# Folding two modulation rows and a gate by adding transfers instead of by sums with ones on TensorE

## Chip, core and metric

One core of one Trainium2 chip runs the program once. The metric is the device time of that run in microseconds (us); for the kernel before it is the median of three runs. The core's engines are TensorE (PE in the profile; its weight loads are PEld), VectorE (DVE), ScalarE (ACT), GpSimd (POOL) and SyncE (SP). Each has its own list of instructions; transfers (DMA) are issued from SP's, ACT's and POOL's lists and move on 16 DMA engines.

## The reference, cut to what matters

A transformer-like layer on 1024 tokens of width 1024 with 256 context tokens, all in float32:

```
mod = silu(c) @ w_mod + b_mod            # one row of 6 * 1024 numbers
sh1, sc1, gt1, sh2, sc2, gt2 = split(mod, 6)
h  = rmsnorm(x, g_pre_mix) * (1 + sc1) + sh1
u, q, k, v = h @ w_in                    # pooling half and attention half
mix = concat(pool_mixer(u), neighbourhood_attention(q, k, v)) @ w_out
x  = x + gt1 * rmsnorm(mix, g_post_mix)
h2 = rmsnorm(x, g_pre_mlp) * (1 + sc2) + sh2
y  = square(relu(h2 @ w_mlp_in)) @ w_mlp_out
out = x + gt2 * rmsnorm(y, g_post_mlp)
```

The rows `gt1`, `sh2`, `sc2` and `gt2` are the ones named "a", "sh", "sc" and "b" in the kernel. Each is a product of a vector of 1024 with a 1024x1024 matrix.

## The kernel before

The products are made of float32 numbers split into a high and a low part (`split`, `high_low`), three matmuls for one (`three`, L226 to L228), and the large products are put together from fewer products of sums of blocks (P1 to P7). In order of time: modulation of the first sub-layer and projection (to about 210 us), attention in 32 units of a head pair and eight columns of tokens (`units`, to about 313 us), the output projection (to about 390), the first MLP product (block pairs `block_pair(p)`, p from 0 to 15, to about 700), the second MLP product (to the end).

**How a modulation row is made.** `mod_begin` takes a page of 128x1024, sets it to zero and loads the bias into its first partition. Eight parts of `w_mod` are loaded, and VectorE adds each, times one column of silu(c), into the page (`mod_add`, L251). The page `acc` then holds for each of the 1024 outputs 128 partial sums, one in each partition, and these have still to be added up. `mod_sums_of` does this on TensorE: four matmuls with a matrix of ones (L264), each for 256 outputs, so that the sums of a quarter stand in 32 partitions of a bank of PSUM. What follows differs:

- "a" and "b", the gates: VectorE multiplies the sums by the gain (`mod_gate`, L275), whose quarters four transfers bring to the same partitions (`mod_gain`, L271). `mod_out` (L281) writes the row to DRAM in four transfers, and `gate_page` (L287) reads it back into all 128 partitions: `Ga` and `Gb`.
- "sc" and "sh", scale and shift of the second sub-layer: ScalarE copies the sums (`column_sums`, L847), `mod_out` writes four quarters, and `columns_of` (L850) reads the row back as 8 columns of 128, into `sc2` and `s2`. From these VectorE makes `a2`, `less_a2` and `less_s2` (L1752 to L1754), which `normal_pair` and `normal_sides` (L1774, L1798, L1800) use on the transposed tokens.

The shift's page is stored to DRAM (`kept_row`, L842) after its last part and loaded into a new page at the first unit of attention (L1489). The sums of "a" and of both modulation rows stand in unit 2 of the attention loop; the transfers out are jobs of units 5 and 6, those of columns jobs of units 10 and 12. The sums of "b" stand ahead of group 3 of the second MLP product's P1; its parts are added in block pairs 10 to 12.

**What sets the order.** A planner orders the instructions of each engine: from its own estimate of times it takes, of those whose inputs are ready, the one that stands first in the program, and it chooses the buffers. `in_order(engines)` fixes the order on the engines named, as written, for what is inside. The attention part and the transfers behind it are such a list on POOL (`first_pool`); the second part of the output projection, from the row steps on, is another (`added`), and nothing ties the two lists to each other. `tc.issue_after(i)` only sets what follows behind instruction i on its own engine. Adding transfers (`add_to`: DRAM or SBUF plus what stands there) are issued from POOL's list. A transfer that needs an earlier one's result waits in its engine's list for that to land.

**Around the change, in the output projection.** POOL's list has: the sums of pairs of weight blocks (`t2`, whose tiles are named to_2w and to_3w, as those of `t3` and `t4`), one sum of head outputs, two adding transfers into `t3` and two into `t4`. Then come the row steps of the first four token tiles: VectorE adds two partial mean squares (`vm`), POOL takes the power -1/2 (`rm`, L168), VectorE makes the new row (L1670), ScalarE its square, POOL a second power (`rn`), and VectorE the scaled row `mp` (L1683), which TensorE transposes (`px`, L1765) for the MLP. `wt3` and `wt4` are the split blocks of `t3` and `t4`.

Of the kernel before, what the change touches and what calls it, by code (L numbers as in the profile page):

```python
# [11 lines left out]
F32 = mybir.dt.float32  # L12
# [6 lines left out]
P = 128  # L19
D = 1024  # L20
KT = D // P
# [87 lines left out]
def hybrid_block(ctx, tc, x, ctx_in, w_mod, mod_pages, w_u, b_mod, gp1, gp2, w_in, pool_w, rpb, w_out, w1, w2, vectors,  # L109
                 mask, edge, out):  # L110
    nc = tc.nc
    sub, mul, add = ALU.subtract, ALU.mult, ALU.add
# [6 lines left out]
    dram = ctx.enter_context(tc.tile_pool(name="dram", bufs=1, space=DRAM))  # L119

    def cst(name, shape, dt=F32):
        return const.tile(shape, dt, tag=name, name=name)
# [4 lines left out]
    def page(name, dt=F32):  # L127
        return act.tile([P, 1024], dt, tag="pg", name=name)
# [85 lines left out]

    def add_to(to, more):
        nc.gpsimd.dma_start(to, more, accum_op=add)  # L216

    def pair(w, kk, c0, n):
        return w[2 * kk * P : (2 * kk + 2) * P, c0 : c0 + n].rearrange("(a p) f -> p a f", p=P)
# [41 lines left out]
    def mod_sums_of(name, acc, bank):  # L261
        ps = bank(f"pg{name}")
        for c in range(4):
            nc.tensor.matmul(ps[32 * c : 32 * c + 32, :256], ones[:, :32], acc[:, c * 256 : (c + 1) * 256],  # L264
                             start=True, stop=True)
        return ps[:, :256]

    def mod_gain(gp, g, queue):
        quarters = gp.rearrange("(c o f) -> c o f", c=4, o=1)
        for c in range(4):  # L270
            queue.dma_start(g[32 * c : 32 * c + 32, :], quarters[c].to_broadcast([32, 256]))  # L271
        return g

    def mod_gate(name, acc, g, bank):
        nc.vector.tensor_tensor(acc[:, :256], mod_sums_of(name, acc, bank), g, mul)  # L275


    def mod_out(name, acc):
        gates[name] = dram.tile([1, D], F32, tag=f"g{name}", name=f"g{name}")
        for c in range(4):  # L280
            nc.gpsimd.dma_start(gates[name][:, c * 256 : (c + 1) * 256], acc[32 * c : 32 * c + 1, :256])  # L281

    gates = {}
# [13 lines left out]
    a2, s2 = cst("a2", [P, KT]), cst("s2", [P, KT])  # L297

    with tc.tile_pool(name="ps1", bufs=6, space=PSUM) as ps1, tc.tile_pool(name="tmp1", bufs=3) as tmp:

        def bank(name):
            if name[:2] == "pm" or name in ("pxt5", "pxb2", "pxb3", "pxb4", "pxb5", "pcs", "pcr"):
                return lasting(name)
            return ps1.tile([P, 512], F32, tag="mm", name=name)
# [526 lines left out]
        accs = {}  # L831


        kept_row = dram.tile([P, D], F32, tag="row", name="row")

        def mod_parts(name, c, n):
            accs[name] = mod_begin(name, c, page)
# [5 lines left out]
                yield  # L843


        def column_sums(name, acc, bank):
            nc.scalar.copy(acc[:, :256], mod_sums_of(name, acc, bank))  # L847

        def columns_of(name, to):
            nc.gpsimd.dma_start(to, gates[name].rearrange("o (k p) -> p (o k)", p=P))  # L850

        scale2 = cst("sc2", [P, KT])
        rest.append(mod_parts("sh", 3, KT))
# [372 lines left out]
    with (  # L1226
# [217 lines left out]
        with in_order(ET.PE, ET.Activation, ET.DVE, ET.SP) as projected:  # L1444
# [16 lines left out]
            def right_added(j):  # L1461
# [4 lines left out]
            built = lambda j: next(table[j])  # L1466
            out_of = lambda n: mod_out(n, accs[n])
            jobs = {0: [(built, 1), (key_parts, 1, 0), (key_parts, 1, 1)], 1: [(built, 1)], 2: [(built, 1)], 3: [(built, 1)],
                    4: [(built, 1)], 5: [(out_of, "a"), (out_of, "sc")], 6: [(out_of, "sh")], 7: [(query_parts, 1, 1, True, True)],
                    8: [(mixed_split, 0, True)], 9: [(built, 2)],  # L1470
                    10: [(columns_of, "sc", scale2), (built, 2)], 12: [(columns_of, "sh", s2), (built, 2)],
                    13: [(built, 2), (built, 2)], 14: [(query_parts, 3, 0, False, True)],
                    16: [(mixed_split, 1, True)], 17: [(query_parts, 2, 1, True, True)],
                    18: [(built, 3), (key_parts, 3, 0, False, True)], 20: [(built, 3), (built, 3)],
# [4 lines left out]
            for i in range(N):  # L1479
                if i in LOADS:  # L1480
                    weight_load(0, kks[LOADS.index(i)])
                if i == N - 2:
                    G1 = gate_page("a")
                if i > 3:
                    weighed(i - 4)
                if i == 0:
                    gain = mod_gain(gp1, att.tile([P, 256], F32, tag="gp", name="gpa"), nc.sync)
                    accs["sh"] = page("accsh2")
                    nc.sync.dma_start(accs["sh"], kept_row)  # L1489
                if i == 2:  # L1490
                    mod_gate("a", accs["a"], gain, rest_of_bank)
                if i in (5, 6):
                    for k in (2 * i - 10, 2 * i - 9):
                        nc.sync.dma_start(sa2[k], s3[k])
                low()
                scores(i)
                biased(i, 0)
                if i < N - 1:
                    biased(i, 1)
                if 8 < i and i % 8 == 3:  # L1500
                    right_added(i // 8 - 1)
                if 8 < i and i % 8 == 7:
                    add_to(heads[i // 8 - 1][:, :512], sa2[i // 8 - 1])
                for f, *args in jobs.get(i, ()):
                    f(*args)
                if block_copies and (i < 4 or 6 < i):
                    block_copied()
                for _ in range(SUMS.count(i)):
                    block_summed()
                if i == 2:  # L1510
                    late_query = part_page("qP0_1", False)
                    qparts[0, 1] = late_query[:, :512], late_query[:, 512:]
                    high_part(qT[0][1], qparts[0, 1][0])
                if i > 1:
                    turn(i - 2)
                    fifth_kept(i - 2)
                if i == 2:
                    turn_kept(0, 0, nc.scalar.copy)
                    column_sums("sc", accs["sc"], lambda name: pa[:, :256])
                if i == N - 1:  # L1520
                    turn_kept(i - 2, 0, nc.scalar.copy)
                    turn_kept(i - 2, 1, nc.vector.tensor_copy)
                    biased(i, 1)
                exps(i, 0)
                if i == 2:
                    column_sums("sh", accs["sh"], rest_of_bank)
                if 2 < i < N - 1:
                    turn_kept(i - 2, 0, nc.scalar.copy)
                exps(i, 1)
                if i == 0:  # L1530
                    key_parts(2, 0, True, "lo")
                    key_parts(2, 1, True, "lo")
                    query_parts(2, 0, False, "lo")
                if 1 < i < N - 1:
                    turn_kept(i - 2, 1, nc.vector.tensor_copy)
                if i == 2:
                    low_part(qT[0][1], *qparts[0, 1])
                for filler in fillers.get(i, ()):
                    last_query(*filler)
                if i > 2:  # L1540
                    values(i - 3)
# [60 lines left out]
            for i in range(2):  # L1602
                add_to(t2[i], t1[i])
            add_to(heads[3][:, :512], sa2[3])
            for i in range(2):
                add_to(halved(t3[i]), out_block(i, 1))
            for i in range(2):
                add_to(t4[i], t2[i])
            first_pool.__exit__(None, None, None)
            wt1 = [high_low(f"to1_{t}", t1[t]) for t in range(2)]  # L1610
            junk = lambda t: att.tile([P, NKEY], F32, tag="sp", name=f"jo0_{t}", bufs=6)[:, :512]
# [10 lines left out]
    with tc.tile_pool(name="ps2", bufs=6, space=PSUM) as ps2:  # L1622
# [6 lines left out]
      with ExitStack() as tmp2:  # L1629
# [119 lines left out]

        less_a2, less_s2 = sm("na2", 8), sm("ns2", 8)  # L1750
        with tc.issue_after(projected[ET.DVE]):
            nc.vector.scalar_tensor_tensor(a2, scale2, 1.0, g2c, add, mul)  # L1752
            nc.vector.tensor_scalar_mul(less_a2, a2, -1.0)
            nc.vector.tensor_scalar_mul(less_s2, s2, -1.0)  # L1754
# [521 lines left out]
        with in_order(ET.Pool):  # L2276
            for p in range(1, NPAIR - 1):
                block_pair(p, lambda: acc_b.extend(islice(row_b, 1 if p >= EARLY else 0)))
        assert next(row_b, None) is None
        first_order.__exit__(None, None, None)  # L2280
        fixed.append(True)
        with tc.issue_after(first[ET.PE]), in_order(ET.PE, ET.Activation, ET.DVE, ET.SP, ET.Pool):
# [65 lines left out]
                ending.append((m, gated(m, h, src, True), xt))  # L2348


            pg = bank("pgb")
            inner_banks, parts = {}, {}
            by_two = lambda v: v.rearrange("p (t n) -> p t n", t=2)

# [48 lines left out]
            for name, g in items[: items.index(("P6", 0))]:  # L2403
                if name[0] == "M":
                    inner_group(name, g)
                elif name == "P1":
                    if g == 1:
                        gain = mod_gain(gp2, page("gpb")[:, :256], nc.gpsimd)
                    if g == 3:
                        mod_gate("b", acc_b[-1], gain, lambda name: pg)  # L2410
                        mod_out("b", acc_b[-1])
                    group(x, "P1", g)
                    if g == NG - 1:
                        s1 = halves("s1")
                        for t in range(4):
                            nc.scalar.copy(s1[t], x[t])
                else:
                    group(x, "P2", g, more=True)
                    if g == NG // 2:
                        G2 = gate_page("b")  # L2420
# [110 lines left out]
```

## Time and profile before

| | |
|---|---|
| runs | 1010.14, 1011.23, 1011.56 us; median 1011.23 |
| profiled execution | 1010.35 us, span 1008.6 us |
| TensorE's granted clock | 0.998 of full speed |
| DMA queues | q1 (issued by SP) 181.63 MB, q0 (by POOL) 38.45 MB, q10 (by ACT) 30.97 MB |

The profile shows one execution. The span runs from the first to the last instruction. A row of a timeline has the start, the duration, engine, line, operation, the tile written and those read (`out<-in`, buffer numbers left out), the shape and a count; in brackets the idle time before it and what ended it. In the chain, the work that ended last is followed back, and its pieces don't overlap. "Landing" is the time from a transfer's issue until its data have arrived. The names of tiles: pa, pz and pgb are PSUM banks, S the scores, accsc, accsh and accb the pages of partial sums, gsc and gsh the rows in DRAM, rb the reciprocals of the softmax sums.

### The profile page before, as it was taken

The numbers are of one execution on the slowest core, as the hardware profiler recorded it, in microseconds if no ns is written. First come the engines' busy times: TensorE is split into PE (matmuls) and PEld (weight loads), VectorE is DVE, ScalarE is ACT, GpSimd is POOL, SyncE is SP. The second block draws the span as 40 slices with busy tenths as digits, with TensorE's granted clock in tenths as the row PEclk, the third lists the DMA queues.
The fourth block names the chain that finished last, engine by engine and source line by source line (L and its number), as shares of the span: only waits on it lengthen the run. The fifth ranks groups of instructions, "written<-read, shape, count | busy, mean of one in ns | idle before, by whom it ended". The sixth has DMA issues, their size and how long they took to land.

```text
span 1008.6 us, 16695 instructions
## 1 busy us (share of the span) xinstructions
PE 997.9 (99%) x6062; PEld 829.4 (82%) x6062; DVE 798.6 (79%) x1276; ACT 581.0 (58%) x1038; POOL 201.9 (20%) x278
## 2 busy tenths in 40 slices
PE   8999999999999999999999999999999999999997
PEld 5788888878998888888888888888888888888886
DVE  5589766968885689879998888754798888888895
ACT  6673254448886746786555544545556565544551
POOL 4111110166985232410000000000001000021121
PEclk9999999999999999999999999999999999999999
DMA  9999798665989979986776666625999999579944
GB/s 362 396 278 340 237 273 306 219 160 194 230 184 249 238 191 274 297 208 205 261 252 217 201 215 221 213 89 184 333 371 300 286 341 322 171 220 315 318 166 162
DMA packets 146882, 252.10 MB, mean 250 GB/s; under 512 B 10417, under 2 KB 76849, under 8 KB 146801
## 3 DMA queue, kind: packets, MB, share of 16 engines
q1 hardware_dynamic: 111024, 181.63, 52.9%
q0 software_dynamic: 18640, 38.45, 19.8%
q10 hardware_dynamic: 17136, 30.97, 8.3%
q8 instruction: 47, 0.77, 0.3%
q14 instruction: 35, 0.28, 0.1%
HBM read 197.52 MB, written 69.22 MB: 264 GB/s over the span
## 4 chain that ended last, share of the span: by engine, by line
PE 96%; DVE 1%; DMA 1%; ACT 1%; issue 0%; POOL 0%; SPq 0%; DVEq 0%; POOLq 0%; ACTq 0%
PE pu L481 5%; PE pyiM L2394 4%; PE pyiN L2394 4%; PE pa L1342 4%; PE S L1255 3%; PE phx L226 3%; PE phz L226 3%; PE phv L226 3%; PE pyx L226 3%; PE pyx L227 3%; PE pyx L228 3%; PE phx L228 3%; PE phz L228 3%; PE phv L228 3%; PE phx L227 3%; PE phv L227 3%
## 5 line engine op out<-in xcount | busy, mean ns | idle before, releaser
L1962 ACT ACTIVATE c<-c 128x512 f32<-128x512 f32 x48 | 30.3, 631 | 44.2 <-DVE c L2084 25.3
L174 ACT CAST wpS<-S 128x512 fp32r<-128x512 f32 x64 | 38.7, 617 | 28.6 <-PE phv L228 10.1
L1286 ACT ACTIVATE sp<-sp,nm 128x640 f32<-128x640 f32 (+1 forms) x64 | 51.4, 804 | 6.1 <-DVE ri L1290 5.0
L1275 DVE CUSTOM_DVE_ANT_0 sp<-S,tab 128x640 f32<-128x640 f32 (+1 forms) x56 | 44.5, 795 | 13.0 <-PE pz L1308 9.8
L226 PE MATMUL phx<-thB,wpA 128*128 128x512 f32 x128 | 50.2, 392 | 0.0
L180 DVE TENSOR_TENSOR wpS<-S,wpS 128x512 fp32r<-128x512 f32 x64 | 43.4, 686 | 8.2 <-ACT wpS L174 8.2
L228 PE MATMUL phx<-thB,wpA 128*128 128x512 f32 x128 | 49.8, 389 | 0.0
L227 PE MATMUL phx<-tlB,wpA 128*128 128x512 f32 x128 | 49.8, 389 | 0.0
L216 POOL DMA_DIRECT2D t<-in_w x16 | 19.3, 1207 | 105.8 <-PE pyx L228 31.8
L1963 ACT ACTIVATE c<-c 128x512 f32<-128x512 f32 x48 | 30.3, 630 | 15.8 <-DVE sa L2047 12.1
L243 POOL MEMSET accb<- 128x1024 f32 x1 | 1.0, 958 | 142.1 <-ACT c L1963 142.1
L226 PEld LDWEIGHTS phx<-thB,wpA 128*128 128x128 f32 x128 | 24.0, 188 | 5.4 <-ACT s L2015 0.4
L228 PEld LDWEIGHTS phx<-thB,wpA 128*128 128x128 f32 x128 | 24.0, 188 | 5.1
L227 PEld LDWEIGHTS phx<-tlB,wpA 128*128 128x128 f32 x128 | 24.0, 188 | 4.9
L1342 PE MATMUL pa<-pt,v 128*64 128x128 f32 x352 | 25.8, 279 | 0.0
L226 PE MATMUL phz<-thB,wpS 128*128 128x512 f32 x64 | 25.0, 391 | 0.0
L226 PE MATMUL phv<-thT,wpA 128*128 128x512 f32 x64 | 25.0, 391 | 0.0
L228 PE MATMUL phz<-thB,wpS 128*128 128x512 f32 x64 | 24.9, 389 | 0.0
L228 PE MATMUL phv<-thT,wpA 128*128 128x512 f32 x64 | 24.9, 389 | 0.0
L227 PE MATMUL phv<-tlT,wpA 128*128 128x512 f32 x64 | 24.9, 389 | 0.0
L226 PE MATMUL phy<-thT,wpS 128*128 128x512 f32 x64 | 24.9, 389 | 0.0
L227 PE MATMUL phy<-tlT,wpS 128*128 128x512 f32 x64 | 24.9, 389 | 0.0
(1191 smaller groups left out, 3568.8 us busy)
## 6 DMA issues: line engine op xcount, KB each, us to landing
hrA<-hdA SPq DMA_DIRECT2D x24, 512.0 KB, 7.3
wm<-in_mod_pages SPq DMA_DIRECT2D x16, 512.0 KB, 9.3
wa_0w<-in_w SPq DMA_DIRECT2D x16, 512.0 KB, 4.8
wa_1w<-in_w SPq DMA_DIRECT2D x16, 512.0 KB, 4.3
hdA<-c ACTq DMA_DIRECT2D x32, 256.0 KB, 2.3
hdS<-sa ACTq DMA_DIRECT2D x32, 256.0 KB, 3.0
hqS<-sb ACTq DMA_DIRECT2D x32, 256.0 KB, 3.9
b<-in_w SPq DMA_DIRECT2D x16, 512.0 KB, 8.3
```

Of the source, the lines that this page charges most:

```text
L174: nc.scalar.copy(hi, src)
L180: nc.vector.tensor_tensor(lo, src, hi.bitcast(F32), sub)
L226: nc.tensor.matmul(ps, ahi, bhi, start=first, stop=False, skip_group_check=more)
L227: nc.tensor.matmul(ps, ahi, blo, start=False, stop=False, skip_group_check=more)
L228: nc.tensor.matmul(ps, alo, bhi, start=False, stop=last, skip_group_check=more)
L481: nc.tensor.matmul(pus[b][j], wk(wgt, k, low, j * P, P), r, start=(k == 0 and n == 0), stop=(k == KT - 1 and n == 2))
L1275: nc.vector.tensor_tensor_reduce(out=to, in0=s, in1=bt, scale=1.0, scalar=BIG, op0=add, op1=ALU.min, accum_out=nm)
L1286: nc.scalar.activation(sp, sp, AF.Exp, bias=least[i, e], scale=-1.0, accum_out=sums[i][:, e : e + 1])
L1342: nc.tensor.matmul(pa[e * HD : (e + 1) * HD, cols], v[:, f : f + HD], turns[i][:, e, c] if c < 4 else fifths[i][:, :, (e + 1) * HD : (e + ...
L1962: nc.scalar.activation(r, src, AF.Relu)
L1963: nc.scalar.activation(r, r, AF.Square)
L2394: nc.tensor.matmul(to, a[part][:, j * 256 + t * P : j * 256 + (t + 1) * P], r, start=h + j == 0 and n < 2, stop=ends and n > 1)
```

## The change

The sums with ones of "sc", "sh" and "b" go, with their copies, quarters and reads; "a" stays as it was.

- Scale and shift: the shift's page stays in DRAM; the scale's page is stored there as well at the first unit, and the shift's is no longer loaded. The DRAM tile is 256 wider than the 1024 that are used. Behind the attention loop, in POOL's list `first_pool`, adding transfers fold the 128 rows within DRAM: rows 64 to 127 onto 0 to 63, then 32, 16, 8 and 4 onto as many, for both rows by turns (`both_folded`). Four rows are left, and each is loaded as columns into `four_rows` (`columns_loaded`, eight transfers). VectorE adds the four with two sums for each (`columns_of`), ahead of `a2`.
- The second gate: seven adding transfers fold the page in SBUF down to one partition, at block pair 13. The gain is loaded as one row, POOL multiplies the two rows in one partition, and one transfer writes the row to DRAM. The PSUM bank `pgb` isn't taken.

```diff
+    def rows_folded(rows, *counts):
+        for n in counts:
+            add_to(rows[:n], rows[n : 2 * n])
...
-        kept_row = dram.tile([P, D], F32, tag="row", name="row")
+        kept_row = dram.tile([P, D + 256], F32, tag="row", name="row")[:, :D]
...
-        def column_sums(name, acc, bank):
-            nc.scalar.copy(acc[:, :256], mod_sums_of(name, acc, bank))
+        kept_rows = {"sh": kept_row}
+        four_rows = {n: cst(f"four{n}", [P, 4, KT]) for n in ("sc", "sh")}
+
+        def both_folded(*counts):
+            for n in counts:
+                for rows in kept_rows.values():
+                    rows_folded(rows, n)
+
+        def columns_loaded():
+            for n, rows in kept_rows.items():
+                for r in range(4):
+                    nc.gpsimd.dma_start(four_rows[n][:, r], rows[r : r + 1].rearrange("o (k p) -> p (o k)", p=P))
 
         def columns_of(name, to):
-            nc.gpsimd.dma_start(to, gates[name].rearrange("o (k p) -> p (o k)", p=P))
+            four = four_rows[name]
+            nc.vector.tensor_tensor(four[:, :2], four[:, :2], four[:, 2:], add)
+            nc.vector.tensor_tensor(to, four[:, 0], four[:, 1], add)
...
-   jobs 5: (out_of, "a"), (out_of, "sc"); 6: (out_of, "sh"); 10 and 12: columns_of
+   jobs 5: (out_of, "a")
...
                 if i == 0:
-                    accs["sh"] = page("accsh2")
-                    nc.sync.dma_start(accs["sh"], kept_row)
+                    kept_rows["sc"] = dram.tile([P, D + 256], F32, tag="rowsc", name="rowsc")[:, :D]
+                    nc.sync.dma_start(kept_rows["sc"], accs["sc"])
...
                 if i == 2:
                     turn_kept(0, 0, nc.scalar.copy)
-                    column_sums("sc", accs["sc"], lambda name: pa[:, :256])
...
-                if i == 2:
-                    column_sums("sh", accs["sh"], rest_of_bank)
...
             add_to(heads[3][:, :512], sa2[3])
+            both_folded(64, 32)
             for i in range(2):
                 add_to(halved(t3[i]), out_block(i, 1))
             for i in range(2):
                 add_to(t4[i], t2[i])
+            both_folded(16, 8, 4)
+            columns_loaded()
...
         with tc.issue_after(projected[ET.DVE]):
+            columns_of("sc", scale2)
+            columns_of("sh", s2)
             nc.vector.scalar_tensor_tensor(a2, scale2, 1.0, g2c, add, mul)
...
                 block_pair(p, lambda: acc_b.extend(islice(row_b, 1 if p >= EARLY else 0)))
+                if p == NPAIR - 3:
+                    rows_folded(acc_b[-1], *(1 << n for n in range(6, -1, -1)))
...
-            pg = bank("pgb")
...
                     if g == 1:
-                        gain = mod_gain(gp2, page("gpb")[:, :256], nc.gpsimd)
+                        gain = page("gpb")[:1]
+                        nc.gpsimd.dma_start(gain, gp2.rearrange("(o d) -> o d", o=1))
                     if g == 3:
-                        mod_gate("b", acc_b[-1], gain, lambda name: pg)
-                        mod_out("b", acc_b[-1])
+                        nc.gpsimd.tensor_tensor(acc_b[-1][:1], acc_b[-1][:1], gain, mul)
+                        gates["b"] = dram.tile([1, D], F32, tag="gb", name="gb")
+                        nc.gpsimd.dma_start(gates["b"], acc_b[-1][:1])
```

More of the change, by code (lines that the diff above doesn't have):

```diff
@@ L1468, in hybrid_block @@
             jobs = {0: [(built, 1), (key_parts, 1, 0), (key_parts, 1, 1)], 1: [(built, 1)], 2: [(built, 1)], 3: [(built, 1)],
-                    4: [(built, 1)], 5: [(out_of, "a"), (out_of, "sc")], 6: [(out_of, "sh")], 7: [(query_parts, 1, 1, True, True)],
+                    4: [(built, 1)], 5: [(out_of, "a")], 7: [(query_parts, 1, 1, True, True)],
                     8: [(mixed_split, 0, True)], 9: [(built, 2)],
-                    10: [(columns_of, "sc", scale2), (built, 2)], 12: [(columns_of, "sh", s2), (built, 2)],
+                    10: [(built, 2)], 12: [(built, 2)],
                     13: [(built, 2), (built, 2)], 14: [(query_parts, 3, 0, False, True)],
@@ L2278, in hybrid_block @@
                 block_pair(p, lambda: acc_b.extend(islice(row_b, 1 if p >= EARLY else 0)))
+                if p == NPAIR - 3:
+                    assert len(acc_b) == KT + 1
+                    rows_folded(acc_b[-1], *(1 << n for n in range(6, -1, -1)))
         assert next(row_b, None) is None
```

## The prediction, made before the changed kernel was run

> **What bounds the kernel now.** I read the page first, for the engine that is full, then the chain of waits, then the timelines of the two places that the change touches.
>
> ```profile
> PE 997.9 (99%) x6062; PEld 829.4 (82%) x6062; DVE 798.6 (79%) x1276; ACT 581.0 (58%) x1038; POOL 201.9 (20%) x278
> PE 96%; DVE 1%; DMA 1%; ACT 1%; issue 0%; POOL 0%; SPq 0%; DVEq 0%; POOLq 0%; ACTq 0%
> ```
>
> TensorE is busy for 99% of the span and carries 96% of the chain. So time taken out of TensorE's own list comes off the end, as long as everything that feeds it keeps up; time on another engine counts only where TensorE then waits.
>
> **The sums with ones.** The chain and TensorE's timeline around them:
>
> ```profile
> 225.60 0.64 PE L264 MATMUL pa<-accsc,ones 128*32 128x256 f32 x8
> ...
> 226.60 0.68 PE L1255 MATMUL S<-kP0h,qP 64*128 64x384 f32 x2
> ...
> 229.86 0.44 PE L1255 MATMUL S<-kP0h,qP 64*128 64x384 f32 x2
> ...
> 232.87 0.44 PE L1255 MATMUL S<-kP0h,qP 64*128 64x384 f32 x2
> ```
> ```profile
> 721.66 0.57 PE pgb L264 x8
> ```
>
> The group reads as 0.64 us, but groups overlap in this view; what counts is start to start, and the shift row's group lies between the two lines. The scale and shift rows hold TensorE from 225.60 to 226.60: 1.00 us. The second gate's row takes 0.57 us of the chain, whose pieces don't overlap. All of it is on the path, because TensorE's next work directly follows. **Term one: -1.57 us.** Only the first gate's sum ("a") stays.
>
> **What hung on them in the attention loop.** Each sum was copied by ScalarE, and each row written out by four transfers from GpSimd's queue:
>
> ```profile
> 226.30 0.03 ACT accsc L847
> ...
> 226.57 0.92 ACT sp L1286 x2
> 227.49 0.26 ACT accsh L847
> 227.76 0.82 ACT sp L1286 x2
> ```
> ```profile
> 237.67 1.91 POOL L281 DMA_DIRECT2D gsc<-accsc  x4
> 239.58 0.30 POOL L1292 COPY rb<-ri 128x128 f32<-128x128 f32 x1
> ```
> ```profile
> 238.88 0.39 PE L1255 MATMUL S<-kch,qP 64*128 64x256 f32 x2
> ...
> 242.01 0.39 PE L1255 MATMUL S<-kch,qP 64*128 64x256 f32 x2
> ...
> 245.08 0.44 PE L1255 MATMUL S<-kP1h,qP 64*128 64x384 f32 x2
> ```
>
> Here the chain leaves TensorE: from 226.30 to 228.58 it runs through ScalarE and both copies. The unit that begins at 226.60 lasts 229.86 - 226.60 = 3.26 us, the next 232.87 - 229.86 = 3.01. With the copies gone I take the difference, 0.25 us. At 237.67 the scale row's four transfers stand ahead of the copy rb, which TensorE's transposes of that unit need; the unit at 238.88 lasts 3.13 us and the one at 242.01 3.07. One head pair later the same two places last 2.84 and 2.96:
>
> ```profile
> 262.63 0.39 PE L1255 MATMUL S<-kch,qP 64*128 64x256 f32 x2
> ...
> 265.47 0.38 PE L1255 MATMUL S<-kch,qP 64*128 64x256 f32 x2
> ...
> 268.43 0.44 PE L1255 MATMUL S<-kP2h,qP 64*128 64x384 f32 x2
> ```
>
> That is 0.29 + 0.11 = 0.40 us. **Term two: -0.65 us**, between 0 (another wait, such as VectorE's, ends last there instead) and 0.65. I take the whole, since both chains run through the removed work by name.
>
> **What costs nothing, and its cover.** The scale row now goes out by one store from SyncE where the shift row came in by one load of the same 512 KB, in an idle stretch of its queue:
>
> ```profile
> 201.12 0.36 SPq L1489 DMA_DIRECT2D accsh<-row  x1
> 214.64 1.48 SPq L1101 DMA_DIRECT2D U<-in_rpb  x2
> ```
>
> The cost is 0; uncovered, it would be one load's time. One page fewer is claimed, which can only free a buffer sooner. The second gate's row is folded by seven adding transfers in series on GpSimd's queue, after its last part on VectorE:
>
> ```profile
> 627.84 1.28 DVE L251 SCALAR_TENSOR_TENSOR accb<-wmb_7w,sx,accb 128x1024 f32<-128x1024 f32 x1 [1.26 <-DMA wmb_7w<-in_w_mod]
> 694.53 1.99 POOL L271 DMA_DIRECT2D gpb<-in_gp  x4 [111.39 <-PE phz L228]
> 782.90 0.32 SPq L287 DMA_DIRECT2D Gb<-gb  x1
> ```
> ```profile
> y<-y POOLq DMA_DIRECT2D x4, 256.0 KB, 5.7
> f<-ss POOLq DMA_DIRECT2D x4, 256.0 KB, 10.0
> ```
>
> By the median landings of two 256 KB adding transfers, at 5.7 us a level seven levels are 40 us, at 10.0 us 70 us: done between 669 and 699, where GpSimd is idle for 111 us and the row is not read back until 782.90. The product with the gain moves from VectorE to GpSimd (one partition, 1024 elements: an estimated 2.4 us, eight times the 0.30 that rb takes for 128), and one row store replaces four. Even the worst sum leaves some 80 us, less GpSimd's own wait for the page at 694.53. Nothing waits: 0. Without that cover it would be the whole chain.
>
> **The folds of scale and shift: the open cost.** They go on GpSimd's queue into the output projection: two pairs (64 and 32 rows) ahead of the transfers that add into t3, three pairs (16, 8, 4) behind those into t4, then eight loads of columns. Each level waits on GpSimd for the level before it to land, and everything behind it waits too. What stands there now:
>
> ```profile
> 336.13 1.20 POOL L216 DMA_DIRECT2D f<-ss  x1
> 336.67 1.91 POOL L216 DMA_DIRECT2D to_2w<-in_w_out  x1
> ...
> 343.19 0.86 POOL L216 DMA_DIRECT2D to_3w<-to_3w  x1 [1.76 <-DMA to_3w<-to_1w]
> 367.51 1.01 POOL L168 TENSOR_TENSOR rm<-vm,nhalf 128x1 f32<-128x1 f32 x1 [23.47 <-DVE vm L166]
> ```
>
> Two landings, of the transfer of 336.13 and of the one of 343.19 (the view of a tile, cut to one transfer):
>
> ```profile
> DMA to landing us min/median/max: 8.2/8.2/8.2
> ```
> ```profile
> DMA to landing us min/median/max: 11.4/11.4/11.4
> ```
>
> What reads t3 and the columns on ScalarE, what VectorE does there, the transposes that follow in the chain; then the landings of accb's tile and the one column load of before:
>
> ```profile
> 359.64 1.05 ACT L174 CAST to_0h<-to_2w 128x1024 fp32r<-128x1024 f32 x1 [4.11 <-PE poy L227]
> ...
> 388.87 1.45 ACT L1774 ACTIVATE nf<-px,s,a 128x512 f32<-128x512 f32 x2 [2.88 <-PE px L1765]
> ```
> ```profile
> 343.24 0.16 DVE L1752 SCALAR_TENSOR_TENSOR a<-sc,cols 128x8 f32<-128x8 f32 x1
> ...
> 387.30 0.75 DVE L1683 TENSOR_SCALAR mp<-xr,rn 128x1024 f32<-128x1024 f32 x1 [0.45 <-POOL rn L168]
> ```
> ```profile
> 388.39 0.87 PE px L1765 x8
> ```
> ```profile
> DMA to landing us min/median/max: 2.3/5.0/5.1
> ```
> ```profile
> 250.75 0.95 POOL L850 DMA_DIRECT2D sc<-gsc  x1 [0.28 <-issue]
> ```
>
> GpSimd has 23.5 us free from 344 to 367.51, and the columns are first used by ScalarE at 388.87. If the first two levels need 10 us together, t3 is added about 10 us later than 336.67 and, with the 10.0 us of the row above, lands near 357, still ahead of its cast at 359.64. So two deadlines are left: rm at 367.51 and the columns at 388.87.
>
> The price of the chain. The transfer of 336.13 lands at 336.1 + 8.2 = 344.3, the last into t4 at 343.2 + 11.4 = 354.6, four transfers later: the queue is backed up and moves on by 2.6 us a transfer of 512 KB. So the top level lands at about 346, the next some 4 us later at 350, and the four transfers into t3 and t4 at about 361; the three small levels at 2 to 3 us, so 367 to 370; eight column loads at 0.5 to 1.0 us of issue each (four of gsc's rows took 1.91 above, the one column load of before 0.95), so 373 to 377. That is 5.5 to 9.5 us past 367.51. The other end is a queue without backlog: each level at about the 2.3 us of the smallest single load (the bias row into accb, the least of its tile's landings), which ends the columns near 359 and costs nothing.
>
> Whether the late end hurts depends on the order. GpSimd's lists of the attention part and of the projection's second part are each fixed by hand, but not against each other; between them the planner puts first what is ready first. The trace shows it doing so: L1752 is written after all the row steps and ran at 343.24, ahead of them. In the same way rm, released by VectorE at 367.5, can pass column loads that are still waiting; then 20 us are left for the columns until 388.87. I take that: **0**, range 0 to +9; a gain is excluded, since nothing is taken off GpSimd's queue between 334 and 389. VectorE's four short sums of columns are at about 0.16 us each (L1752), 0.7 us in a stretch with 3.85 us free:
>
> ```profile
> 367.00:389.00 22.00, 22.00 (x103) 18.28 (x102) 18.15 (x31) 10.31 (x22) 15.07 (x17) 1.00 0.91 212
> ```
>
> The Trainium skill, "DMA: Bandwidth & Descriptors", in the section on the anatomy of one DMA on the SWDGE path, gives about 2.0 us plus bytes over 436 GB/s for a transfer from GpSimd. By that a 256 KB fold would take an estimated 2.6 us and the chain would end before 360, the same sum as mine. The trace disagrees with it here: the 256 KB rows above took 5.7 and 10.0 us. The same section says that a transfer's wait is held on the issuing sequencer; the trace agrees (the 1.76 us of GpSimd ahead of 343.19).
>
> **Sum.** -1.57 - 0.65 + 0 = -2.2 us. The profiled execution took 1010.35 us, 1.75 more than its span, and stands 0.88 under the median of the three runs, 1011.23. Against the median: **1009.0 us**, -0.22%. I take 0.2%, 2.0 us, as what a measurement of this kernel tells from no change.
>
> **Rivals.**
> 1. *GpSimd is held in written order* (slower). If the planner believes the folds shorter than they are, all column loads stand ahead of rm, or VectorE's sums stand ahead of row work, and wait there for landings. From rm the chain runs without slack to the scaled rows: the last is done at 387.30 + 0.75 = 388.05, and TensorE transposes it at 388.39 (0.34 us free). So 5.5 to 9.5 us late at rm cost 5.2 to 9.2: 1009.0 + 5.2 = 1014.2, to 1018.2. For it: the 5.7 to 10 us landings and the eight loads; against it: the freedom of order. It decides once the columns end more than 2.5 us past rm's time (0.34 and the 2.2 gained).
> 2. *Only the matmuls come off.* The attention units are then held by VectorE or ScalarE, or a stall of 1 to 2 us in the projection eats part: 1011.23 - 1.57 = 1009.7, up to 1011.7. For it: VectorE is 79% busy, and term two is a sum of three small differences.
> 3. *It does nothing on the path*, if the ones sums ran in TensorE's waiting time. Against it: TensorE's busy share; 1011.2, under 5%, and counted with rival 2.
>
> **How the numbers follow.** Forecast 0.50 (1008.2 to 1009.7), rivals 2 and 3 0.20, rival 1 0.30. Of the forecast's half two thirds lie under 1009.2, and a little comes from luckier sums: faster 0.36; the rest with rivals 2 and 3: same 0.34; slower 0.30. The range from 1007.9 (the profiled execution's 0.88 under the median, applied again, and 0.2) to 1017.0 leaves out the tail of rival 1 and little below.
>
> **What would show it.** Right: TensorE's L264 only at 223; units of 3.0 and 2.85 us where 3.26 and 3.13 stood; rm's wait still for VectorE; no gap at the transposes of 388. Wrong: on GpSimd, waits of 5 us and more for row or four ahead of rm; on VectorE, a wait for a load ahead of the sums of columns; a gap of TensorE before px or pov between 372 and 389. For the second gate: Gb's load later than its old place in the order.

## The result, and the profile after

The changed kernel took 1027.80 us (median of 4 runs, 1026.55 to 1029.04) against 1010.98 for the kernel before (4 runs): a ratio of 1.017, interval 1.0158 to 1.0182, some 17 us slower. The profiled execution took 1026.55 us, its span 1024.8. The page's busy line and its chain, of the changed kernel:

```profile
PE 999.6 (98%) x6038; PEld 831.1 (81%) x6038; DVE 799.3 (78%) x1279; ACT 580.1 (57%) x1036; POOL 216.7 (21%) x288
PE 85%; DMA 8%; DVE 3%; issue 2%; POOL 1%; SPq 0%; ACT 0%; DVEq 0%; POOLq 0%; ACTq 0%
```

TensorE has 24 instructions fewer, yet its share of the chain falls from 96% to 85%, and DMA has 8% where it had 1%: somewhere the end now hangs on transfers. The windows view finds the place. Its columns after the stretch are its length, the busy time of each engine with its instructions, the granted clock, the DMA share and GB/s. The stretch shown before as full, of the changed kernel:

```profile
367.00:389.00 22.00, 13.16 (x51) 10.50 (x50) 9.57 (x21) 3.21 (x8) 13.11 (x15) 0.77 0.39 85
```

TensorE works 13.16 of 22.00 us where it worked all 22.00, and the DMA engines move 85 GB/s in place of 212: everything stands. The chain in order of time, of the changed kernel, says what for:

```profile
350.14 12.18 DMA row<-row
...
368.39 4.12 DMA row<-row
...
372.80 2.74 POOL foursh L861 x3
375.54 2.97 DMA foursh<-row
...
379.23 1.22 DVE to_0l L180
380.44 0.72 DVE to_1l L180
...
384.17 1.02 POOL rm L168
...
405.08 0.87 PE px L1783 x8
```

The folds of the shift's row, its column loads, then VectorE's work that stood behind them, then rm. From rm to the transposes px it is 405.08 - 384.17 = 20.91 us, and before it was 388.39 - 367.51 = 20.88: the whole of the loss (px 16.69 us later) has happened by rm (16.66 later). The lists of the two engines that meet there, VectorE's and GpSimd's timelines of the changed kernel:

```profile
361.00 0.68 DVE L1719 TENSOR_TENSOR so<-poy,so 128x512 f32<-128x512 f32 x1
378.53 0.18 DVE L865 TENSOR_TENSOR foursh<-foursh 128x16 f32<-128x16 f32 x1 [16.84 <-DMA foursh<-row]
378.62 0.69 DVE L1720 TENSOR_TENSOR so<-so,so 128x512 f32<-128x512 f32 x1
379.23 1.22 DVE L180 TENSOR_TENSOR to_0l<-to_2w,to_0h 128x1024 fp32r<-128x1024 f32 x1
...
383.93 0.15 DVE L166 SCALAR_TENSOR_TENSOR vm<-ssm,ssm 128x1 f32<-128x1 f32 x1
```
```profile
336.80 1.49 POOL L216 DMA_DIRECT2D row<-row  x1
...
345.80 0.78 POOL L216 DMA_DIRECT2D row<-row  x1 [6.70 <-DMA row<-row]
...
362.61 0.81 POOL L216 DMA_DIRECT2D row<-row  x1 [8.83 <-DMA row<-row]
...
368.39 0.79 POOL L216 DMA_DIRECT2D row<-row  x1 [4.14 <-DMA row<-row]
...
372.80 3.63 POOL L861 DMA_DIRECT2D foursh<-row  x4 [2.54 <-DMA row<-row]
376.41 3.51 POOL L861 DMA_DIRECT2D foursc<-rowsc  x4
384.17 1.01 POOL L168 TENSOR_TENSOR rm<-vm,nhalf 128x1 f32<-128x1 f32 x1 [4.25 <-DVE vm L166]
```

The planner put the first column sum (L865) between two steps of VectorE's output work, long ahead of the row steps, and VectorE stood there 16.84 us. The step behind the wait (L1720 at 378.62) is L1704 in VectorE's timeline of the kernel before:

```profile
361.95 0.69 DVE L1704 TENSOR_TENSOR so<-so,so 128x512 f32<-128x512 f32 x1
```

In the changed kernel it comes 16.67 us later, and so does all that follows on VectorE, up to vm. On GpSimd all folds and all eight column issues stand ahead of rm, until 376.41 + 3.51 = 379.92; then rm still waited 4.25 us for vm. So in this run VectorE came last, and its wait is the whole loss. GpSimd's list was 12.4 us late too (379.92 against 367.51), but hidden behind VectorE's wait. What each list does without the other, and whether the transfers slow others, is for the experiments.

The earlier place, unit 2 of the attention loop: TensorE's timeline of the changed kernel, then VectorE's of the kernel before and of no_rows (below), where the sums are gone too.

```profile
226.02 0.44 PE L1271 MATMUL S<-kP0h,qP 64*128 64x384 f32 x1 [0.36 <-DVE nm L1291]
...
229.60 0.60 PE L1271 MATMUL S<-kP0h,qP 64*128 64x384 f32 x2
...
232.77 0.44 PE L1271 MATMUL S<-kP0h,qP 64*128 64x384 f32 x2
...
238.77 0.39 PE L1271 MATMUL S<-kch,qP 64*128 64x256 f32 x2
...
241.61 0.38 PE L1271 MATMUL S<-kch,qP 64*128 64x256 f32 x2
...
244.44 0.44 PE L1271 MATMUL S<-kP1h,qP 64*128 64x384 f32 x2
```
```profile
226.70 0.08 DVE L1275 DVE_READ_ACCUMULATOR2_ANT nm<- 128x1 f32 x1
...
228.10 0.81 DVE L1275 CUSTOM_DVE_ANT_0 sp<-S,tab 128x640 f32<-128x640 f32 x1
```
```profile
226.74 0.08 DVE L1291 DVE_READ_ACCUMULATOR2_ANT nm<- 128x1 f32 x1
...
228.15 0.81 DVE L1291 CUSTOM_DVE_ANT_0 sp<-S,tab 128x640 f32<-128x640 f32 x1
```

The unit that began at 226.60 begins at 226.02, but the next ones at 229.60 (229.86 before) and 232.77 (232.87 before). TensorE now waits for VectorE's nm, and VectorE's rows are at the same times with the sums and without them (226.70 and 226.74, 228.10 and 228.15): VectorE set the pace of this unit all along, and all but 0.1 us of the sums with ones (232.87 against 232.77) ran in time that TensorE would have waited.

### The profile page after: what moved, and what is told of

Read it like the earlier page. It is cut to its first block, busy times and chain, and to the rows that moved or that the text cites. A ratio compares the mean times of both kernels' runs of the same rounds, so it can differ in the third digit from the quotient of the medians.

```text
span 1024.8 us, 16644 instructions
## 1 busy us (share of the span) xinstructions
PE 999.6 (98%) x6038; PEld 831.1 (81%) x6038; DVE 799.3 (78%) x1279; ACT 580.1 (57%) x1036; POOL 216.7 (21%) x288
## 4 chain that ended last, share of the span: by engine, by line
PE 85%; DMA 8%; DVE 3%; issue 2%; POOL 1%; SPq 0%; ACT 0%; DVEq 0%; POOLq 0%; ACTq 0%
PE pu L485 4%; PE pyiM L2414 4%; PE pa L1358 4%; PE S L1271 3%; PE phx L230 3%; PE phv L230 3%; PE phz L230 3%; PE pyx L231 3%; PE pyx L230 3%; PE phx L231 3%; PE phz L232 3%; PE phv L232 3%; PE phx L232 3%; PE pyx L232 3%; PE phz L231 3%; PE phv L231 3%
## 5 line engine op out<-in xcount | busy, mean ns | idle before, releaser
L230 PE MATMUL phv<-thT,wpA 128*128 128x512 f32 x64 | 25.0, 391 | 0.0
L231 PE MATMUL phz<-tlB,wpS 128*128 128x512 f32 x64 | 24.9, 389 | 0.0
```

What stands on the lines that cost most here:

```text
L230: nc.tensor.matmul(ps, ahi, bhi, start=first, stop=False, skip_group_check=more)
L231: nc.tensor.matmul(ps, ahi, blo, start=False, stop=False, skip_group_check=more)
```

## The experiments

Theories: V, VectorE's place makes the loss (the wait of 16.84 us). G, GpSimd's list makes it (rm behind the columns). T, the folds' traffic slows other transfers. All times are medians, with the kernel before on the same chip beside them.

**b_only.** Scale and shift as before; only the second gate's part of the change.

> Before, with the second gate's fold alone; scale and shift keep their sums with ones on TensorE. If the two halves of the change are independent and the loss is all in the output projection, this gains what the changed kernel gained at pyx, 0.73 us less the 0.25 us that it lost again at the end: 0.5 to 0.7 us, a time of 1010.3 to 1010.5. If fold traffic as such slows other transfers, the 24 us of levels between 646 and 677 us would show here too and the time would be at or above 1011.

1009.63 us against 1010.22, ratio 0.9993 (0.9984 to 1.0002; the interval includes no change). The loss is not here, as every theory but T had it. The row was folded and multiplied while GpSimd had nothing else; GpSimd's timeline of the changed kernel:

```profile
646.22 0.82 POOL L216 DMA_DIRECT2D accb<-accb  x1 [46.40 <-DVE accb L255]
...
675.27 0.79 POOL L216 DMA_DIRECT2D accb<-accb  x1 [4.08 <-DMA accb<-accb]
711.21 0.53 POOL L2429 DMA_DIRECT2D gpb<-in_gp  x1 [35.15 <-PE phz L232]
714.40 2.95 POOL L2431 TENSOR_TENSOR accb<-accb,gpb 1x1024 f32<-1x1024 f32 x1 [2.66 <-DMA gpb<-in_gp]
```

**sums_late.** VectorE's place alone is mended:

```diff
 # in the list `added`, behind row_second(3)
+            columns_of("sc", scale2)
+            columns_of("sh", s2)
+            (a2, less_a2, less_s2)
...
-        with tc.issue_after(projected[ET.DVE]):
-            columns_of("sc", scale2)
-            columns_of("sh", s2)
```

> The changed kernel, with the column sums and the three steps that follow them moved in VectorE's list to behind the last row step (row_second(3)); GpSimd's list and all transfers stay. Theory 1 (VectorE's place alone made the loss: it stood 16.84 us at the column sum): the wait goes, px starts near 388 and the time is about 1009.6. Rival (GpSimd's list is enough by itself: rm stands behind eight column issues that end at 379.9): rm starts at 379.9 in place of 367.5, 12.4 us late, px is near 400 and the time 1022 to 1023, only 4 to 5 us better than the changed kernel.

1021.99 us against 1010.22, ratio 1.0118 (1.0104 to 1.0132): the rival's number. VectorE no longer waits for the columns; it waits for GpSimd, whose list ends its column issues at 377.55 + 3.50 = 381.05. VectorE's and GpSimd's timelines of sums_late:

```profile
381.70 1.29 DVE L1686 SCALAR_TENSOR_TENSOR xr<-mp,rm,xr 128x1024 f32<-128x1024 f32 x1 [12.92 <-POOL rm L168]
```
```profile
377.55 3.50 POOL L861 DMA_DIRECT2D foursc<-rowsc  x4
381.07 0.59 POOL L168 TENSOR_TENSOR rm<-vm,nhalf 128x1 f32<-128x1 f32 x1
```

So GpSimd's list is enough for about 12 us, which the changed kernel had hidden behind VectorE's longer wait. Taking the longer of two overlapping waits away gained only the difference, some 5 us. That VectorE's place is enough by itself, with GpSimd's list free, is still to be shown (spread).

**cols_sp.** As sums_late, and the column loads are issued by SyncE (`nc.sync.dma_start` in `columns_loaded`), behind the four row loads; SyncE's order is fixed in the list `added` for it.

> As sums_late, and the eight column loads are issued on SP's queue, behind the four row loads, in place of GpSimd's; the folds stay where they are. If what holds the row steps is each engine's own list, rm now stands only behind the last fold's issue (370.3 against 367.5): px 2.1 to 2.9 us after that of before less 0.7, time 1012 to 1013.5. If the folds' traffic itself slows the row work or the weights, the time stays above 1016. If only the column issues on GpSimd mattered, 1009.6.

1024.05 us against 1010.22, ratio 1.0135 (1.0121 to 1.0149): missed by more than 10 us. The number is that of the second alternative (above 1016), but not for its reason, slower row work or weights. The first half came as expected: with only the folds ahead of it, rm started at 370.60. But SyncE needed 20.9 us to issue eight loads that took GpSimd 7.1, and VectorE, at its new place, waited for them ahead of the last scaled row. SyncE's and VectorE's timelines of cols_sp:

```profile
372.45 11.90 SPq L861 DMA_DIRECT2D foursh<-row  x4
384.51 8.99 SPq L861 DMA_DIRECT2D foursc<-rowsc  x4
```
```profile
397.75 0.17 DVE L865 TENSOR_TENSOR foursc<-foursc 128x16 f32<-128x16 f32 x1 [9.14 <-DMA foursc<-rowsc]
```

**early.** All folds inside the attention loop and the columns right behind it, in an idle stretch of GpSimd:

```diff
-            both_folded(64, 32)
...
-            both_folded(16, 8, 4)
-            columns_loaded()
...
+ jobs 6: both_folded(64); 10: both_folded(32); 15: both_folded(16); 23: both_folded(8); 27: both_folded(4)
+            columns_loaded()
             right_added(3)
```

> The changed kernel with its folds spread through the attention loop (64 rows in unit 6, 32 in unit 10, 16 in unit 15, 8 in unit 23, 4 in unit 27) and the eight column loads right after the loop, in the 8 us in which GpSimd is idle there; nothing else is moved by hand. If the loss is only lateness of the columns, no engine waits for them, px starts 0.6 us before that of before and with the second gate's gain the time is 1009.3 to 1010.0. If GpSimd's ten more issues in the loop (about 1 us each where its list is full, between 255 and 290) make TensorE wait for rb, up to 3 us of it come back: 1010 to 1013.

1018.30 us against 1010.22, ratio 1.0083 (1.0070 to 1.0097): worse than either number. The folds in units 15, 23 and 27 cost about 2 us in the loop, as the second expectation had it; those in units 6 and 10 cost nothing. Most of the rest is the columns: four of the eight issues waited for older transfers in the queue, and what stands behind them in GpSimd's list went out late: y<-f, one operand of the output projection, at 334.65 where the changed kernel has it at 323.08, and the adding transfer to_3w<-to_1w at 339.88 (335.72). The chain runs through the latter, which took 9.81 us to land, to a stop of TensorE of 3.65 us from 346.96. GpSimd's and TensorE's timelines of early:

```profile
333.77 0.89 POOL L861 DMA_DIRECT2D foursc<-rowsc  x1 [4.11 <-DMA foursh<-row]
334.65 0.96 POOL L216 DMA_DIRECT2D y<-f  x1
...
339.88 0.85 POOL L216 DMA_DIRECT2D to_3w<-to_1w  x1 [0.66 <-DMA to_3w<-in_w_out]
```
```profile
350.61 0.77 PE L230 MATMUL poz<-to_0h,S 128*128 128x512 f32 x1 [3.65 <-DVE foursc L865]
```

An idle engine is no free place if its queue is full.

**spread_late and spread.** The folds go where GpSimd's list has room; the two kernels differ in VectorE's place alone.

```diff
+ jobs 6: both_folded(64); 10: both_folded(32)
+            both_folded(16)
             right_added(3)
+            both_folded(8)
...
-            both_folded(64, 32)
+            both_folded(4)
...
-            both_folded(16, 8, 4)
             columns_loaded()
 # spread_late only: columns_of and what follows behind row_second(3), as in sums_late
```

> The changed kernel with its folds moved to where GpSimd had room: 64 rows in unit 6 and 32 rows in unit 10 of the attention loop (places that cost nothing when the folds were spread through the loop), 16 rows right after the loop, 8 rows behind right_added(3), 4 rows ahead of t3 and t4, the eight column loads behind t4; and VectorE's column sums behind row_second(3). Theory (each of the two lists costs what stands in it behind a late transfer, and nothing else does): the columns are issued by 358 to 361, rm is not held, px starts 0.3 to 0.9 us before that of before, and with the second gate's gain the time is 0.9 to 1.5 us below before. Rival (a fold among the transfers of the output weights delays them, whatever waits for the fold): px starts 2 us or more later than that of before, and the time is above before.

> As spread_late, but the column sums stand where the order of VectorE was planned from their operands, as in the changed kernel: here between the first and the second S<-y of the output operands, at about 346 us. GpSimd's list and all transfers are those of spread_late, so this is VectorE's place alone. Theory: VectorE stands there until foursh's columns land (355 to 362), 9 to 16 us, TensorE runs out of operands, and the time is 9 to 16 us above spread_late. Rival (VectorE's place is harmless once GpSimd's row steps are free): the time of spread_late within 1 us.

spread_late took 1010.45 us against 1010.19, ratio 1.0002 (0.9993 to 1.0011): the loss is gone, without the gain that was expected. spread took 1021.82, ratio 1.0113 (1.0098 to 1.0129), 11.4 us more. GpSimd was free in it 22 us before rm came; VectorE alone was late. VectorE's and GpSimd's timelines of spread:

```profile
360.98 0.17 DVE L865 TENSOR_TENSOR foursh<-foursh 128x16 f32<-128x16 f32 x1 [9.60 <-DMA foursh<-row]
...
364.38 0.18 DVE L865 TENSOR_TENSOR foursc<-foursc 128x16 f32<-128x16 f32 x1 [2.23 <-DMA foursc<-rowsc]
```
```profile
380.59 1.01 POOL L168 TENSOR_TENSOR rm<-vm,nhalf 128x1 f32<-128x1 f32 x1 [22.46 <-DVE vm L166]
```

So V is a cause by itself as well: VectorE's two waits for columns, 9.60 and 2.23 us, are what was lost, and they are shorter than the 16.84 of the changed kernel because the columns landed earlier here. GpSimd's list alone made 12 us (sums_late). With neither list held, and the same folds, loads and sums, nothing was lost against before, which leaves T, for the folds at these places, less than the 1 us that spread_late misses of the gain.

**no_rows.** The ceiling.

> The ceiling: the changed kernel without the folds, the column loads and the column sums of scale and shift; that part of the computation is left out (both are set to zero by two small memsets on VectorE). Sums with ones of scale and shift are gone from the loop, the second gate's fold is there. By the prediction's terms this is 2.2 us below before; by what the changed kernel showed (0.69 us at the last unit, 0.73 at pyx, 0.25 lost at the end), 1.2 us below it, because in unit 2 TensorE waits 0.36 us twice for VectorE's nm in place of the sums.

1009.42 us against 1010.19, ratio 0.9993 (0.9985 to 1.0002): 0.77 us, and the interval includes nothing. Beside b_only's 0.59 it leaves about 0.2 us for the scale's and shift's sums, less than the intervals can tell from nothing. The attention loop shows 0.2 to 0.5: from the score matmul that begins at 223.96 in the kernel before to the one at 309.18, 85.22 us, it took 85.01 in b_only, 84.80 in no_rows and 84.54 in the changed kernel. Of the prediction's 2.2 us some 0.8 were there to be had, by the medians.

**spread_mid.** As spread_late, with the column sums at the end of the row loop.

> As spread_late, with the column sums and the three steps after them moved up in VectorE's list, from behind row_second(3) to the end of the row loop, where VectorE is idle 2.16 us before to_0l of the fourth weights. By then the columns have landed (last issue at 356.8 in spread_late). If spread_late's 0.41 us between px and pyx came from these seven small steps standing ahead of row_scaled(3), that part goes and the time is that of no_rows within 0.3 us: 1009.4 to 1009.8. If it came from something else, the time stays near 1010.4.

1009.50 us against 1010.31, ratio 0.9989 (0.9980 to 0.9998): as expected, and the one version of the folds that is below before, by 0.8 us. It is level with no_rows within the intervals: the folds are then free, and theory T falls for these places. At the places of the changed kernel nothing shows it either: there the weights t3 were cast at 359.00, where the kernel before has 359.64. Its stretch of the windows view is full again:

```profile
367.00:389.00 22.00, 22.00 (x103) 18.32 (x102) 19.04 (x37) 10.98 (x23) 15.12 (x17) 1.00 0.94 222
```

**cols_late.** The changed kernel's folds, the column loads among the row steps:

```diff
                 if t > 0:
                     row_added(t - 1)
+                if t == 3:
+                    next(column_loads)          # four of the shift
...
             row_added(3)
+            next(column_loads)                  # four of the scale
...
             row_scaled(3)
+            columns_of("sc", scale2)
+            ...
```

> The changed kernel with its folds where they are, the column loads of the shift behind the third row's store and those of the scale behind the fourth's on GpSimd's list, and the column sums behind row_scaled(3) on VectorE's. If a list costs only what stands in it, rm is at about 370.5 as in cols_sp (2.9 us late for the folds), the first four issues fall into 3.67 us in which GpSimd waits for vm, the other four hold the last rn by about 2 us, and the time is 3 to 6 us above before: 1013 to 1016. If column loads anywhere near the row work cost as much as on SP's queue, 1020 or more.

1022.70 us against 1010.31, ratio 1.0118 (1.0105 to 1.0132): missed. rm was at 369.91, and the last scaled row waited 2.35 us for rn, as expected. What was not: the scale's columns, issued by 390.84, landed at 398.80, and ScalarE's work on px stood for them. The view of the tiles foursh and foursc gives the times to landing; of foursc in the changed kernel, then in cols_late:

```profile
DMA to landing us min/median/max: 2.9/2.9/3.0
```
```profile
DMA to landing us min/median/max: 8.1/8.5/9.0
```

The same loads of 4 KB each. The DMA engines were nearly idle in the first kernel and full in the second (0.29 and 1.42 by the DMA column, 5 and 246 GB/s; 0.97 to 1.21 in the next three windows of the second), by the windows view of each:

```profile
376.00:380.00 4.00, 0.00 (x0) 0.00 (x0) 1.47 (x3) 0.00 (x0) 3.92 (x5) 0.50 0.29 5
```
```profile
384.00:388.00 4.00, 3.88 (x18) 2.88 (x17) 4.00 (x8) 2.63 (x7) 3.42 (x5) 1.00 1.42 246
```

Most of that load was GpSimd's own: between 380 and 392 the packets of its queue took 89.9% of the engines' time, those of SyncE's 25.7%. Its store x<-xr of 512 KB, issued just ahead of the scale's columns at 385.72, took 9.7 us to land as well.

## Why the prediction was wrong

- **Sign and size.** 1009.0 us was forecast, with 1007.9 to 1017.0; it was 1027.8. Rival 1 happened, at a chance of 0.30, and its price of 5.2 to 9.2 us above 1009.0 was half of the 18.8 that came, or less.
- **The step that failed: VectorE's four sums, taken at "0.7 us in a stretch with 3.85 us free".** The prediction added up how long the sums work, and asked only of GpSimd what stands behind a wait. The work was as short as forecast, but the first sum stood 16.84 us until its columns had landed, and VectorE's output and row steps stood behind it: 16.66 us at rm. The prediction took from L1752 that the planner puts first what is ready first, and read it as safety. The row can be read the other way: L1752 is written late and ran at 343.24, so the planner moves such steps forward as far as it believes their inputs to be there. Here it believed the columns there at about 361.7, and they landed at 378.51, at the end of a chain whose five levels took 36 us (336.80 to 372.80); what it estimated for that chain is not on record. That rm "can pass column loads" was wrong too: in the changed kernel it stood behind all eight, which VectorE's wait hid, and in sums_late that cost some 12 us. The signs named for both ("a wait for a load ahead of the sums of columns", "waits of 5 us and more for row or four ahead of rm") are what the profile shows.
- **Why 17 and not 5 to 9.** The rival named both lists but priced only GpSimd's, with rm directly behind the last column issue (373 to 377; measured 379.92). VectorE's wait has another sum: it ended when the first columns had landed, at 378.51, and then 5.4 us of VectorE's work (to_0l, to_1l, the first row's steps) still lay ahead of vm, done at about 384. The two waits overlap, and the longer one counts.
- **The chain's levels.** Forecast: the top level lands by 346, four transfers into t3 and t4 by 361, three levels at 2 to 3 us, done by 367 to 370. Measured: 345.5 by the wait that ended at 345.80; the level of 16 rows, queued behind t3 and t4, took 12.18 us in the chain and landed at 362.3, the next level 5.5 us, the last 4.12, done at 372.5. The shape was right, the last two levels 1 to 3.5 us each too short. By the forecast's own figures the eight column issues (4 to 8 us) end at 371 to 378, not 373 to 377.
- **t3 and t4** were in time, as the prediction had it: the chain's row of to_0l stands behind the columns, not behind a cast.
- **Term one, -1.57 us.** The second gate's 0.57 fits b_only's median of 0.59 us, though its interval includes nothing. Of the 1.00 of scale and shift 0.1 was there: in unit 2 TensorE was at work, but VectorE's nm had the last word. "TensorE's next work directly follows" showed that TensorE was busy, not that VectorE would be ready sooner. The sign of rival 2 ("the attention units are then held by VectorE") was the right one for this part.
- **Term two, -0.65 us.** The 0.25 at ScalarE's copies was not there: that unit lasted 229.60 - 226.02 = 3.58 us, where 3.01 was forecast. The two late units became 2.84 and 2.83 us (238.77, 241.61, 244.44), where 2.84 and 2.96 were forecast. But in b_only, which keeps these transfers, the second of them also lasted 2.84, where the kernel before has 3.07; the first lasted 3.12 there. So 0.28 us of the term are shown as the work of the change. That both chains run through the removed work "by name" was misread for these units: the chain of the kernel before names ga<-acca at this place, a transfer that stayed.
- **The second gate's cover** held: the last fold was issued at 675.27, the product done at 717.35, the row read at 798.86; GpSimd's product took 2.95 us where 2.4 was estimated.

## What to carry to other kernels

When a step that engines share is replaced by a chain of transfers, price the wait and not the work: look up, on every engine that reads the result, what stands behind the first reader in that engine's list, and place the reader by hand where its data have landed and the engine has time (spread_mid). When two engines wait for the same transfers, the waits overlap: the profile shows the longer one, and the other appears only when that is gone. Time taken from the busiest engine counts only where the next wait on its operands is known to end earlier; compare when the other engine's result is ready, not how full the first one looks. A stretch in which an engine is idle is only a place for transfers if its queue and the DMA engines have room then.

## What the runs showed of the hardware

- The landing of small transfers differed with what was under way: 2.9 us at a DMA share of 0.29, 8.5 us at 0.97 to 1.42. The Trainium skill, "DMA: Bandwidth & Descriptors", in the section that issuing engines are not separate DMA queues, says that transfers of all issuers run on the same 16 engines and interleave. The two rows don't test this, since most of the load in the second kernel stood in GpSimd's own queue (89.9% of the engines' time, by the view of cols_late above); no run here separates the two.
- SyncE was held far longer by the issues of eight column loads (20.9 us in cols_sp) than GpSimd (7.1 in the changed kernel, where the DMA engines were nearly idle). In spread_mid, at a DMA share of 1.09, four of GpSimd's issues still took 3.59 us. That the scattered elements of these loads are the reason is not shown: in cols_late one of SyncE's plain row loads (xr<-in_x) held its list for 12.16 us.
- TensorE's granted clock was lower in and behind its long stops. Of the changed kernel, the windows around its longest stop (8.84 us):

```profile
371.00:381.00 10.00, 1.16 (x4) 0.70 (x4) 2.47 (x4) 0.00 (x0) 7.12 (x8) 0.63 0.24 10
381.00:384.00 3.00, 3.00 (x8) 2.34 (x8) 2.97 (x11) 0.72 (x2) 0.00 (x0) 0.51 0.03 0
384.00:387.00 3.00, 3.00 (x15) 2.45 (x14) 2.53 (x5) 1.20 (x3) 2.41 (x3) 1.00 0.00 0
```

TensorE worked at half clock for some 3 us after it started again (0.51 from 381 to 384). Here this cost nothing that can be seen, since px waited for the rows, and rm to px was as long as before. In early it did cost: behind the stop of 3.65 us the clock was 0.53 from 350.7 to 353.6, with TensorE at work all the time, an estimated 1.4 us (0.47 of 2.9 us) on top of the stop.
